# Recurrence output copied out of PSUM at once, its transposes one chunk later

## The chip, the cores and the metric

The kernel runs on one core of a Trainium2 chip. Times are microseconds (us) of one launch on the device. The matrix engine is PE (TensorE), the vector engine DVE, the scalar engine ACT, GpSimd POOL, and SP (SyncE) issues DMAs. The metric is the median of the launch times: 2477.68 us over 3 runs (2475.45 to 2480.0).

## The reference

It is a two-layer encoder trunk on 1024 tokens of width 1024, in float32. Layer 0 mixes by a gated MLP and pooling, layer 1 by RWKV-7; a SwiGLU feed-forward network (FFN) follows each, and a norm ends it. The change lies in RWKV-7, per head of 64:

```
def step(state, inp):                      # one token, 16 heads
    r_t, w_t, k_t, v_t, a_t, b_t = inp
    sa = einsum('bhvk,bhk->bhv', state, a_t)
    state = state * w_t + sa * b_t + v_t * k_t      # outer products
    return state, einsum('bhvk,bhk->bhv', state, r_t)
...
y = wkv7_scan(rh, decay, kh, vh, -kk, kk * ah)
y = (y - mean(y)) * rsqrt(var(y) + GN_EPS)          # per token and head
y = y * ln_w + ln_b + bonus
return (y * g) @ w_o
```

The FFN is `(silu(hn @ w_gate) * (hn @ w_up)) @ w_down`, with a hidden width of 2816.

## The kernel before

The tokens are worked in two halves of 512 (h = 0, 1). Every big product splits both float32 operands into a high and a low part and sums three matmuls: lines 344 to 346 (`mm3`), each 128x128 weights against 512 columns. A weight tile of 512 KB is loaded (`raw`), ACT rounds it to the high part (line 143: `whi`, for the down projection `wdhi`), and DVE subtracts it to get the low part (line 144: `wlo`, `wdlo`). ACT also issues the loads (line 113). One group of the FFN has three hidden tiles: six gate and up tiles of 24 matmuls each, then three down tiles with 72 matmuls together.

The recurrence of a half (`recur`) runs beside an FFN stage of dense matmuls. Eight chunks of 64 tokens follow each other, all heads at once, in small matmuls (line 1176). In the rows, a chunk (`burst`) reads in this order:

- `sm<-XT,w` (`below2`), evicted to `XT` by ACT and DVE;
- `sm<-uv,gt` (`own`), evicted to `akv` by ACT; `sm<-S,ar`, added to `akv` as `Q` by DVE;
- `sm<-ar,bk` (`gram`, two halves for the next chunk), evicted to `gt` by DVE;
- `sm<-Q,XT`, evicted to `uv` by ACT and DVE;
- `yp<-S,ar`, and later `yp<-uv,gt`: the output of the chunk, in PSUM;
- `sm<-uv,bkt`, added to the state by DVE (`Q<-S`, `S`);
- `sm<-ident,bk` (`flip_bk`), evicted to `bkt` by ACT; `sm<-XT,gt` (`below`), evicted to `w` by ACT and DVE.

Two chunks share one PSUM tile `yp` of two banks, and there is one such tile. All `sm` results share three PSUM banks in turn. After every second chunk `post` takes the statistics of `yp` (line 1353), a power on POOL gives the scale, ACT normalizes 16 heads out of `yp` (line 1370), DVE and POOL apply gain and bonus, PE transposes the result (`sm<-ident,ysb`, 1 and then 7), and DVE gates it into `gch` (line 1390), which SP writes out. The small matmuls keep their written order (`ordered`). Where dense matmuls stand between them, and how the work of ACT, DVE and SP is interleaved, is set by a scheduler that runs on its own estimates when the kernel is built; the engines then run their lists in that order.

Of the kernel before, what the change touches and what calls it, by code (L numbers as in the profile page):

```python
# [11 lines left out]
AF = mybir.ActivationFunctionType  # L12
ALU = mybir.AluOpType
# [3 lines left out]
P = 128  # L17
# [19 lines left out]
def tile_trunk(  # L37
# [8 lines left out]
    act, dve, pool, pe, sp = nc.scalar, nc.vector, nc.gpsimd, nc.tensor, nc.sync  # L46
    x = x.flatten_outer_dims()
    out = out.flatten_outer_dims()
# [31 lines left out]
    ident = const.tile([P, P], F32, name="ident")  # L80
# [9 lines left out]
    C_MIX, C_FFN, C_MU, C_W0, C_A0, C_KK, C_KA, C_RK, C_LNB = 0, 16, 32, 80, 88, 96, 104, 112, 120  # L90
# [3 lines left out]
    def col(c):  # L94
        return vec[:, c : c + 1]
# [229 lines left out]
    def pst(tag):  # L325
        t, n = psum["tags"][tag]
        return psum["pool"].tile([P, HT], F32, tag=t, bufs=n, name=t)
# [148 lines left out]
    o = auxt()  # L476
# [675 lines left out]
    def recur(h, wp):  # L1152
# [5 lines left out]
        def wt(tag, bufs, shape):  # L1158
            return wp.tile(shape, F32, tag=tag, bufs=bufs, name=tag)
# [12 lines left out]
        def ordered(f, *args, **kw):  # L1172

            if last:
                with tc.issue_after(last.pop()):
                    i = f(*args, **kw)  # L1176
            else:
                i = f(*args, **kw)
            last.append(i.ins)
# [47 lines left out]
        def flip_bk(c):  # L1227
            bk = C[c][1]
            bkt = wt("bkt", 1, [P, 8, P])
            for q in range(2):  # L1230
                o = pst("sm").rearrange("p (a b) -> p a b", b=P)
                for j in range(4):
                    ordered(pe.transpose, o[:, j, :], bk[:, q * 4 + j].rearrange("p a b -> p (a b)"), ident)
                act.activation(bkt[:, q * 4 : q * 4 + 4, :], o, AF.Copy)
            return bkt
# [41 lines left out]
        def burst(c, bkt, w1):  # L1277

            ar, _, uv, gt, _, XT = C[c]
            cg, S0, more = h * 8 + c, S[0], c < 7  # L1280
            below2(c, w1)
            akv = own(c)
            oq = smt()
            each(oq, lambda r, p: ar[rows[r], p, 0, :], lambda r, p: S0[rows[r], p, :])
            Q = wt("Q", 1, [P, 8, 64])
            dve.tensor_tensor(out=Q, in0=akv, in1=oq, op=ALU.add)
            yield 0.1
            if more:
                gram(c + 1, 0)
                yield 0.1  # L1290
            ou = smt()
            each(ou, lambda r, p: XT[rows[r], p, :], lambda r, p: Q[rows[r], p, :])
            act.activation(uv[rows[0], :, 0, :], ou[rows[0]], AF.Copy)
            dve.tensor_copy(uv[rows[1], :, 1, :], ou[rows[1]])
            yield 0.1
            if c % 2 == 0:
                ypair[0] = psum["pool"].tile([P, 2, 8, 64], F32, tag="y", bufs=1, name="yp")

            yp = ypair[0][:, c % 2]
            for p in range(8):  # L1300
                for r in range(2):
                    mm(
                        yp[rows[r], p, :], ar[rows[r], p, 1, :], S0[rows[r], p, :], start=p == 0, stop=False,
                        skip_group_check=True,
                    )
            yield 0.1
            if more:
                gram(c + 1, 1)
                yield 0.1
            if cg < NCH - 1:  # L1310
                Sn = state_d if c == 7 else wt("S", 2, [P, 8, 64])
                os_ = smt()
                each(os_, lambda r, p: bkt[:, p, r * 64 : r * 64 + 64], lambda r, p: uv[:, p, r, :])
                tS = wt("Q", 1, [P, 8, 64])
                dve.tensor_tensor(out=tS, in0=S0, in1=os_, op=ALU.add)
                dve.tensor_tensor(out=Sn, in0=tS, in1=bc(pct[:, cg, :].unsqueeze(2), [P, 8, 64]), op=ALU.mult)
                S[0] = Sn
                yield 0.1
            for p in range(8):
                for r in range(2):  # L1320
                    mm(
                        yp[rows[r], p, :], gt[:, p, r, 64:128], uv[:, p, r, :], start=False, stop=p == 7,
                        skip_group_check=True,
                    )
            C.pop(c)
            yield 0.1
            if more:
                bkt = flip_bk(c + 1)
                if c < 6:
                    load(c + 2)  # L1330
                yield 0.1
                w1 = below(c + 1)
                yield 0.1
            return bkt, w1

        def post(jj):
            yp = ypair[0]
            j = h * 4 + jj
            gch = wt("gch", 1, [P, 8, P])
            sp.dma_start(gch, g_d[h][:, :, jj * P : (jj + 1) * P])  # L1340
            vch = wt("vch", 1, [P, 2, 8, 64])
            for r in range(2):
                sp.dma_start(
                    vch[rows[r]].rearrange("t c p d -> t c (p d)"),
                    v_d[h][jj * P : (jj + 1) * P, r].rearrange("(c t) p d -> t c (p d)", t=64),
                )
            v16 = vch.rearrange("t c p d -> t (c p) d")
            b16 = bon[:, 2 * j : 2 * j + 2, :].rearrange("t c p -> t (c p)")
            pool.tensor_tensor(out=v16, in0=v16, in1=bc(b16.unsqueeze(2), [P, 16, 64]), op=ALU.mult)
            st = wt("st", 1, [P, 2, 8, 6])  # L1350
            for r in range(2):
                for p in range(8):
                    dve.bn_stats(out=st[:, r, p, :], in_=yp[:, r, p, :])
            sts = st.rearrange("p a b s -> p (a b) s")
            mean, dm, var = (wt(n, 1, [P, 16]) for n in ("mean", "dm", "var"))
            me, mo, ve, vo = (sts[:, :, i] for i in (1, 4, 2, 5))
            dve.tensor_tensor(out=mean, in0=me, in1=mo, op=ALU.add)
            dve.tensor_tensor(out=dm, in0=me, in1=mo, op=ALU.subtract)
            dve.tensor_tensor(out=var, in0=ve, in1=vo, op=ALU.add)
            dve.scalar_tensor_tensor(out=dm, in0=dm, scalar=16.0, in1=dm, op0=ALU.mult, op1=ALU.mult)  # L1360
            dve.tensor_tensor(out=var, in0=var, in1=dm, op=ALU.add)
            dve.tensor_scalar(out=var, in0=var, scalar1=1.0 / 64, scalar2=GN_EPS, op0=ALU.mult, op1=ALU.add)
            rsqrt(var)
            dve.scalar_tensor_tensor(out=mean, in0=mean, scalar=-0.5, in1=var, op0=ALU.mult, op1=ALU.mult)
            yield 0.3
            ysb = wt("ysb", 1, [P, 2, 8, 64])
            for r in range(2):
                for p in range(8):
                    i = r * 8 + p
                    act.activation(  # L1370
                        ysb[:, r, p, :], yp[:, r, p, :], AF.Identity, scale=var[:, i : i + 1], bias=mean[:, i : i + 1]
                    )
            yield 0.3
            for q, eng in enumerate((dve, pool)):
                eng.tensor_tensor(out=ysb[:, q], in0=ysb[:, q], in1=lnw, op=ALU.mult)
                eng.tensor_tensor(out=ysb[:, q], in0=ysb[:, q], in1=vch[:, q], op=ALU.add)
            yield 0.3
            yield 0.3
            for q in range(2):
                o = pst("sm")  # L1380
                for i in range(4):
                    p = 4 * q + i // 2 * 2
                    ordered(
                        pe.transpose, o[:, i * P : (i + 1) * P], ysb[:, i % 2, p : p + 2, :].rearrange("t p d -> t (p d)"), ident
                    )
                ov = o.rearrange("p (q c r t) -> p q r c t", q=2, c=2, r=2)
                for i in range(4):
                    m = q * 4 + i
                    g = gch[:, m, :].rearrange("p (c t) -> p c t", c=2)
                    dve.scalar_tensor_tensor(  # L1390
                        out=g, in0=ov[:, i // 2, i % 2], scalar=col(C_LNB + m), in1=g, op0=ALU.add, op1=ALU.mult,
                    )
                yield 0.5
            sp.dma_start(y_d[h][:, :, jj * P : (jj + 1) * P], gch)

        load(0)
        load(1)
# [8 lines left out]
        for c in range(8):  # L1406
            bkt, w1 = yield from burst(c, bkt, w1)
            yield BURST / 2
            if c % 2 == 1:
                yield from post(c // 2)  # L1410
            yield BURST / 2

    def out_proj(h, ys, after=None):
        for m in range(KT):
# [220 lines left out]
```

## Time and profile before

| | |
|---|---|
| median of 3 runs | 2477.68 us |
| the profiled execution, its own time | 2477.63 us |
| its span, first to last instruction | 2475.9 us |
| PE busy | 2406.4 us, 97% |
| DVE, ACT, POOL busy | 1382.7, 912.1, 244.6 us |
| mean granted clock of PE | 0.989 |

The slices of the page show PE at 9 tenths nearly everywhere. The first recurrence lies at about 933 to 1178 us, the second at about 1640 to 1885 us. A row of a timeline gives the start, the length, the engine, the line, the operation, out<-in, and in brackets how long the engine had been idle and what ended that. Matmuls overlap, so the step from one start to the next is what one costs.

### The profile page before, as it was taken

The page shows a single profiled execution, that of the slowest core. Times are in us where ns is not written, and L with a number is a line of the kernel's source. Part 1 is how long each engine was busy: PE and PEld are TensorE (multiplying, and loading weights), DVE is VectorE, ACT ScalarE, POOL GpSimd, SP SyncE. Part 2 cuts the span into 40 slices and gives each one's busy share as a digit, 9 for nine tenths or more (in the row PEclk, how much of TensorE's full clock was granted, in tenths as well). Part 3 has the DMA queues.
Part 4 walks back from the last instruction along what each step waited for, and adds up shares of the span by engine and source line. Part 5 has one row for each costly group of instructions (what it writes and reads, how often), then busy time and mean ns, then how long its engine had stood idle before and what let it go on. Part 6 is the DMA issues. An engine that isn't in the chain of part 4 may idle for free.

```text
span 2475.9 us, 37980 instructions
## 1 busy us (share of the span) xinstructions
PE 2406.4 (97%) x15735; PEld 1977.5 (80%) x15735; DVE 1382.7 (56%) x2126; ACT 912.1 (37%) x1369; POOL 244.6 (10%) x262
## 2 busy tenths in 40 slices
PE   8999999999999998999999999989999999999998
PEld 7888888888878787888878777778878778888887
DVE  6445634444875874655548847856555446444443
ACT  6233422222664432432325754433232324322223
POOL 0200000000014400211000133201111000000001
PEclk9999999999999999999999999999999999999999
DMA  5123433323355577542434465695444322433231
GB/s 179 49 60 89 150 102 102 119 86 94 109 176 139 140 208 202 156 127 70 135 112 143 153 168 134 191 234 140 119 128 128 111 85 75 147 102 118 87 98 56
DMA packets 436396, 310.69 MB, mean 125 GB/s; under 512 B 93376, under 2 KB 395584, under 8 KB 435456
## 3 DMA queue, kind: packets, MB, share of 16 engines
q10 hardware_dynamic: 297280, 210.53, 28.6%
q1 hardware_dynamic: 138944, 97.75, 13.8%
q8 instruction: 123, 2.02, 0.3%
q14 instruction: 49, 0.40, 0.1%
HBM read 254.68 MB, written 53.54 MB: 124 GB/s over the span
## 4 chain that ended last, share of the span: by engine, by line
PE 82%; DMA 6%; DVE 5%; ACT 2%; issue 2%; POOL 2%; SPq 0%; ACTq 0%; POOLq 0%; DVEq 0%
PE mm L344 22%; PE mm L345 22%; PE mm L346 22%; PE sm L1176 5%; DMA raw<-y_d 1%; DVE wlo L144 1%; PE yp L1176 1%; DMA raw<-in_ffn_w_down_dram 1%; DMA lnw<-in_rwkv_ln_w_dram 1%; ACT whi L143 1%; PE aux L1097 1%; PE mm L511 1%; PE mm L512 1%; PE mm L513 1%; PE aux L1098 1%
## 5 line engine op out<-in xcount | busy, mean ns | idle before, releaser
L345 PE MATMUL mm<-alo,whi 128*128 128x512 f32 x1952 | 766.7, 393 | 0.9 <-issue 0.8
L346 PE MATMUL mm<-ahi,wlo 128*128 128x512 f32 x1952 | 765.4, 392 | 1.7 <-DVE wlo L144 1.7
L344 PE MATMUL mm<-ahi,whi 128*128 128x512 f32 x1952 | 765.8, 393 | 0.8 <-ACT whi L143 0.8
L143 ACT ACTIVATE whi<-raw 128x1024 fp32r<-128x1024 f32 x288 | 304.6, 1059 | 744.7 <-PE mm L345 605.3
L144 DVE TENSOR_TENSOR wlo<-raw,whi 128x1024 fp32r<-128x1024 f32 x288 | 359.1, 1248 | 289.5 <-ACT whi L143 270.1
L346 PEld LDWEIGHTS mm<-ahi,wlo 128*128 128x128 f32 x1952 | 367.7, 188 | 82.5 <-issue 3.5
L345 PEld LDWEIGHTS mm<-alo,whi 128*128 128x128 f32 x1952 | 367.7, 188 | 79.9 <-issue 2.9
L344 PEld LDWEIGHTS mm<-ahi,whi 128*128 128x128 f32 x1952 | 367.7, 188 | 79.0 <-issue 2.1
L344 PE MATMUL mm<-hidhi,wdhi 128*128 128x512 f32 x624 | 240.5, 395 | 8.1 <-DVE h L424 3.8
L345 PE MATMUL mm<-hidlo,wdhi 128*128 128x512 f32 x624 | 245.0, 393 | 0.4 <-DVE hidlo L674 0.4
L346 PE MATMUL mm<-hidhi,wdlo 128*128 128x512 f32 x624 | 244.9, 392 | 0.0
L424 DVE TENSOR_TENSOR h<-h,mm 128x512 f32<-128x512 f32 x192 | 129.3, 686 | 149.7 <-PE mm L346 148.5
L143 ACT ACTIVATE wdhi<-raw 128x1024 fp32r<-128x1024 f32 x82 | 86.4, 1057 | 249.7 <-DMA raw<-in_ffn_w_down_dram 164.4
L144 DVE TENSOR_TENSOR wdlo<-raw,wdhi 128x1024 fp32r<-128x1024 f32 x82 | 100.2, 1223 | 112.1 <-ACT wdhi L143 112.0
L670 DVE TENSOR_TENSOR sg<-sg,mm 128x512 f32<-128x512 f32 x88 | 60.3, 686 | 157.1 <-PE mm L346 155.3
L344 PEld LDWEIGHTS mm<-hidhi,wdhi 128*128 128x128 f32 x624 | 117.5, 189 | 36.8 <-DVE h L424 6.4
L345 PEld LDWEIGHTS mm<-hidlo,wdhi 128*128 128x128 f32 x624 | 117.8, 189 | 25.7 <-DVE hidlo L674 1.3
L346 PEld LDWEIGHTS mm<-hidhi,wdlo 128*128 128x128 f32 x624 | 117.8, 189 | 24.9
L424 DVE TENSOR_TENSOR hA<-hA,mm 128x512 f32<-128x512 f32 x72 | 48.8, 686 | 77.2 <-PE mm L346 77.0
L349 POOL TENSOR_TENSOR nrs<-nrs,small 128x4 f32<-128x4 f32 x8 | 10.0, 1244 | 667.2 <-DVE nrs L371 667.2
L674 DVE TENSOR_TENSOR hidlo<-sg,hidhi 128x512 fp32r<-128x512 f32 x88 | 65.7, 748 | 10.0 <-ACT hidhi L673 10.0
L344 PE MATMUL mm<-xhi,whi 128*128 128x512 f32 (+1 forms) x160 | 65.3, 408 | 0.0
(299 smaller groups left out, 2886.3 us busy)
## 6 DMA issues: line engine op xcount, KB each, us to landing
raw<-in_ffn_w_gate_dram ACTq DMA_DIRECT2D x88, 512.0 KB
raw<-in_ffn_w_up_dram ACTq DMA_DIRECT2D x88, 512.0 KB
raw<-in_ffn_w_down_dram ACTq DMA_DIRECT2D x88, 512.0 KB
raw<-in_ab_w_in_dram ACTq DMA_DIRECT2D x16, 512.0 KB
raw<-in_ab_w_out_dram ACTq DMA_DIRECT2D x16, 512.0 KB
raw<-in_rwkv_w_r_dram ACTq DMA_DIRECT2D x16, 512.0 KB
raw<-in_rwkv_w_k_dram ACTq DMA_DIRECT2D x16, 512.0 KB
ar_d<-ar SPq DMA_DIRECT2D x16, 512.0 KB
```

The costliest lines, as they stand in the source:

```text
L143: act.activation(hi, src, AF.Copy)
L144: (eng or dve).tensor_tensor(out=lo, in0=src, in1=hi.bitcast(F32), op=ALU.subtract)
L344: pe.matmul(o, whi, xhi, start=first, stop=False)
L345: pe.matmul(o, whi, xlo, start=False, stop=False)
L346: pe.matmul(o, wlo, xhi, start=False, stop=last)
L424: dve.tensor_tensor(out=H[h][:, m, :], in0=H[h][:, m, :], in1=o, op=ALU.add)
L511: pe.matmul(ops[j], xhi[:, k, sl], whi[:, kk], start=(k == 0), stop=False)
L512: pe.matmul(ops[j], xhi[:, k, sl], wlo[:, kk], start=False, stop=False)
L513: pe.matmul(ops[j], xlo[:, k, sl], whi[:, kk], start=False, stop=(k == KT - 1))
L670: dve.tensor_tensor(out=s, in0=s, in1=o, op=ALU.mult)
L674: dve.tensor_tensor(out=lo, in0=s, in1=hi.bitcast(F32), op=ALU.subtract)
L1176: i = f(*args, **kw)
```

## The change

`post` begins with two ACT copies that take both halves of `yp` to the SBUF tile `ysb`; statistics and normalization then read `ysb`, and the normalization is in place. The transposes, the gating and the write of `y_d` move to a closure, `turn_out`, which the next chunk calls between `flip_bk` and `below`; the last one is called after the loop. Shortened:

```
             if more:
                 bkt = flip_bk(c + 1)
+                if turned:
+                    turned.pop()()
                 if c < 6:
                     load(c + 2)
...
         def post(jj):
-            yp = ypair[0]
+            ysb = wt("ysb", 1, [P, 2, 8, 64])
+            for r in range(2):
+                act.activation(ysb[:, r], ypair[0][:, r], AF.Copy)
...
-                    dve.bn_stats(out=st[:, r, p, :], in_=yp[:, r, p, :])
+                    dve.bn_stats(out=st[:, r, p, :], in_=ysb[:, r, p, :])
...
-                        ysb[:, r, p, :], yp[:, r, p, :], AF.Identity, scale=var[:, i : i + 1], bias=mean[:, i : i + 1]
+                        ysb[:, r, p, :], ysb[:, r, p, :], AF.Identity, scale=var[:, i : i + 1], bias=mean[:, i : i + 1]
...
-            yield 0.3
-            for q in range(2):
-                o = pst("sm")
...
-                yield 0.5
-            sp.dma_start(y_d[h][:, :, jj * P : (jj + 1) * P], gch)
+            def turn_out():
+                for q in range(2):
+                    o = pst("sm")
...
+                sp.dma_start(y_d[h][:, :, jj * P : (jj + 1) * P], gch)
+            turned.append(turn_out)
...
+        turned.pop()()
+        yield 1.0
```

The number of instructions on PE stays the same. The order of the lists changes from the third chunk of each recurrence on. First PE, end of the seventh chunk of the first recurrence; before:

```order
L1176 MATMUL sm<-uv,bkt 64x64 x16
L1176 MATMUL yp<-uv,gt 64x64 x16
L1176 MATMUL sm<-ident,bk 128x128 x8
L1176 MATMUL sm<-XT,gt 32x32 x16
L345 MATMUL mm<-alo,whi 128x512
```

And with the change, at the same place:

```order
L1176 MATMUL sm<-uv,bkt 64x64 x16
L1176 MATMUL yp<-uv,gt 64x64 x16
L1176 MATMUL sm<-ident,bk 128x128 x8
L1176 MATMUL sm<-ident,ysb 128x128 x4
L346 MATMUL mm<-ahi,wlo 128x512
```

Four transposes of the pair before now follow the flips; 14 dense matmuls, four more transposes, one dense matmul and `sm<-XT,gt` come behind them.

Second ACT, where the loads and splits of the second group's down tiles stand (`raw`, `wdhi`); before, in the sixth chunk:

```order
L1274 ACTIVATE akv<-sm 128x512
L143 ACTIVATE whi<-raw 128x1024
L673 ACTIVATE hidhi<-sg 128x512
L113 DMA raw<-in_ffn_w_down_dram 128x1024
L1293 ACTIVATE uv<-sm 64x8x64
L143 ACTIVATE wdhi<-raw 128x1024
L113 DMA raw<-in_ffn_w_down_dram 128x1024
L143 ACTIVATE wdhi<-raw 128x1024
L1234 ACTIVATE bkt<-sm 128x512 x2
```

With the change, in the seventh chunk:

```order
L1274 ACTIVATE akv<-sm 128x512
L143 ACTIVATE whi<-raw 128x1024
L673 ACTIVATE hidhi<-sg 128x512
L113 DMA raw<-in_ffn_w_down_dram 128x1024
L143 ACTIVATE wdhi<-raw 128x1024
L1293 ACTIVATE uv<-sm 64x8x64
L113 DMA raw<-in_ffn_w_down_dram 128x1024
L143 ACTIVATE wdhi<-raw 128x1024
L113 DMA raw<-in_ffn_w_down_dram 128x1024
L143 ACTIVATE wdhi<-raw 128x1024
L1234 ACTIVATE bkt<-sm 128x512 x2
```

`uv` now stands behind the first down tile's split, and `bkt` behind all three.

Third DVE, the same places; before:

```order
L1223 TENSOR_TENSOR gt<-sm,gm 128x4x128 x2
L1294 COPY uv<-sm 64x8x64
L144 TENSOR_TENSOR wdlo<-raw,wdhi 128x1024
L1223 TENSOR_TENSOR gt<-sm,gm 128x4x128 x2
L1315 TENSOR_TENSOR Q<-S,sm 128x512
L1316 TENSOR_TENSOR S<-Q,pct 128x512
L1353 BN_STATS st<-yp 128x6 x16
L144 TENSOR_TENSOR wdlo<-raw,wdhi 128x1024
```

With the change:

```order
L1223 TENSOR_TENSOR gt<-sm,gm 128x4x128 x2
L144 TENSOR_TENSOR wdlo<-raw,wdhi 128x1024
L1294 COPY uv<-sm 64x8x64
L1223 TENSOR_TENSOR gt<-sm,gm 128x4x128 x2
L144 TENSOR_TENSOR wdlo<-raw,wdhi 128x1024
L1315 TENSOR_TENSOR Q<-S,sm 128x512
L1316 TENSOR_TENSOR S<-Q,pct 128x512
L144 TENSOR_TENSOR wdlo<-raw,wdhi 128x1024
L1397 SCALAR_TENSOR_TENSOR gch<-sm,vec,gch 128x128 x4
```

Here `uv`, the state update `Q<-S` and the gating `gch` each stand behind one more `wdlo`.

## Rows read from the trace of the kernel before

**Rows 1.** The page, part 1: busy time, share of the span, instructions.
```profile
PE 2406.4 (97%) x15735; PEld 1977.5 (80%) x15735; DVE 1382.7 (56%) x2126; ACT 912.1 (37%) x1369; POOL 244.6 (10%) x262
```
**Rows 2.** Stretches of both recurrences: us, busy PE, PEld, DVE, ACT, POOL, PEclk, DMA, GB/s.
```profile
998.00:1178.00 180.00, 177.28 (x2389) 148.09 (x2388) 104.15 (x207) 64.32 (x130) 30.52 (x22) 1.00 0.42 120
1705.00:1885.00 180.00, 174.75 (x2339) 145.28 (x2338) 102.15 (x205) 62.76 (x127) 29.25 (x22) 0.99 0.41 117
```
**Rows 3.** Waits of PE, 998 to 1178: us in total, times, longest us.
```profile
PE sm L1176 <- DVE gt L1223: 1.9, 2, 1.7
```
**Rows 4.** Waits of PE, 1705 to 1885.
```profile
PE sm L1176 <- DVE gt L1223: 2.1, 2, 2.0
...
PE sm L1176 <- DVE ysb L1376: 1.3, 1, 1.3
```
**Rows 5.** Timeline of PE, the fourth chunk of the first recurrence.
```profile
1031.69 0.69 PE L1176 MATMUL sm<-XT,w 32*32 32x32 f32 x32
...
1040.92 1.10 PE L1176 MATMUL yp<-uv,gt 128*64 128x64 f32 x32
1041.96 1.09 PE L1176 MATMUL sm<-ident,bk 128*128 128x128 f32 x8
...
1043.36 0.40 PE L345 MATMUL mm<-alo,whi 128*128 128x512 f32 x1
1043.68 0.69 PE L1176 MATMUL sm<-XT,gt 32*32 32x32 f32 x32
1044.31 0.50 PE L346 MATMUL mm<-ahi,wlo 128*128 128x512 f32 x1
1044.64 0.40 PE L344 MATMUL mm<-ahi,whi 128*128 128x512 f32 x1
1044.87 0.39 PE L345 MATMUL mm<-alo,whi 128*128 128x512 f32 x1
```
**Rows 6.** Timeline of ACT, three down tiles in the second recurrence.
```profile
1793.49 0.60 ACT L1274 ACTIVATE akv<-sm 128x512 f32<-128x512 f32 x1 [0.70 <-PE sm L1176]
...
1797.70 0.35 ACTq L113 DMA_DIRECT2D raw<-in_ffn_w_down_dram  x1
...
1801.51 1.06 ACT L143 ACTIVATE wdhi<-raw 128x1024 fp32r<-128x1024 f32 x1 [2.69 <-DMA raw<-in_ffn_w_down_dram]
1803.85 0.35 ACTq L113 DMA_DIRECT2D raw<-in_ffn_w_down_dram  x1
1808.36 1.06 ACT L143 ACTIVATE wdhi<-raw 128x1024 fp32r<-128x1024 f32 x1 [5.79 <-DMA raw<-in_ffn_w_down_dram]
1810.70 0.33 ACTq L113 DMA_DIRECT2D raw<-in_ffn_w_down_dram  x1
...
1815.63 1.06 ACT L143 ACTIVATE wdhi<-raw 128x1024 fp32r<-128x1024 f32 x1 [3.05 <-DMA raw<-in_ffn_w_down_dram]
```
**Rows 7.** Timeline of DVE, the same place.
```profile
1799.50 0.69 DVE L1294 COPY uv<-sm 64x512 f32<-64x512 f32 x1
1802.60 1.23 DVE L144 TENSOR_TENSOR wdlo<-raw,wdhi 128x1024 fp32r<-128x1024 f32 x1 [2.40 <-ACT wdhi L143]
```
**Rows 8.** Timeline of PE, the same place.
```profile
1804.60 1.25 PE L1176 MATMUL sm<-ident,bk 128*128 128x128 f32 x8 [1.96 <-DVE gt L1223]
...
1807.00 0.63 PE L345 MATMUL mm<-alo,whi 128*128 128x512 f32 x1
1807.43 0.63 PE L346 MATMUL mm<-ahi,wlo 128*128 128x512 f32 x1
```
**Rows 9.** The chain, two other down tiles: start, us, what.
```profile
1090.15 3.54 DMA raw<-in_ffn_w_down_dram
...
1717.66 5.07 DMA raw<-in_ffn_w_down_dram
```
**Rows 10.** Timelines of ACT and DVE: the normalization and one half of the gating.
```profile
1049.45 4.84 ACT L1370 ACTIVATE ysb<-yp,mean,var 128x64 f32<-128x64 f32 x16 [1.89 <-DVE mean L1364]
...
1715.37 1.13 DVE L1390 SCALAR_TENSOR_TENSOR gch<-sm,vec,gch 128x128 f32<-128x128 f32 x4 [0.29 <-PE sm L1176]
```

More of the change, by code (lines that the diff above doesn't have):

```diff
@@ L1334, in burst @@
             return bkt, w1
+        turned = []
         def post(jj):
-            yp = ypair[0]
+            ysb = wt("ysb", 1, [P, 2, 8, 64])
+            for r in range(2):
+                act.activation(ysb[:, r], ypair[0][:, r], AF.Copy)
             j = h * 4 + jj
@@ L1365, in post @@
             yield 0.3
-            ysb = wt("ysb", 1, [P, 2, 8, 64])
             for r in range(2):
@@ L1377, in post @@
             yield 0.3
-            yield 0.3
-            for q in range(2):
-                o = pst("sm")
[L1381 to L1392, printed above, removed]
-                yield 0.5
-            sp.dma_start(y_d[h][:, :, jj * P : (jj + 1) * P], gch)
+            def turn_out():
+                for q in range(2):
+                    o = pst("sm")
+                    for i in range(4):
+                        p = 4 * q + i // 2 * 2
+                        ordered(
+                            pe.transpose, o[:, i * P : (i + 1) * P],
+                            ysb[:, i % 2, p : p + 2, :].rearrange("t p d -> t (p d)"), ident,
+                        )
+                    ov = o.rearrange("p (q c r t) -> p q r c t", q=2, c=2, r=2)
+                    for i in range(4):
+                        m = q * 4 + i
+                        g = gch[:, m, :].rearrange("p (c t) -> p c t", c=2)
+                        dve.scalar_tensor_tensor(
+                            out=g, in0=ov[:, i // 2, i % 2], scalar=col(C_LNB + m), in1=g, op0=ALU.add, op1=ALU.mult,
+                        )
+                sp.dma_start(y_d[h][:, :, jj * P : (jj + 1) * P], gch)
+            turned.append(turn_out)
         load(0)
```

## The prediction

> **What bounds the kernel now.** First the engine totals on the page: PE is busy 97% of the span [rows 1], so a change can gain only where PE stands idle beside the changed code. Next the windows of the two stretches that lie between the end of the first pair and the last `post`: PE is busy for 177.28 and 174.75 of 180 us at a granted clock of 1.00 and 0.99 [rows 2]. That leaves 2.72 + 5.25 = 7.97 us of idle time in both. Then PE's waits in the same stretches: the flips of a chunk, `sm<-ident,bk`, wait for DVE's `gt` for 1.9 and 2.1 us (one long wait in each) [rows 3, 4], and the first transpose of a pair waits 1.3 us for `ysb` [rows 4]. These 5.3 us can be touched; the other 2.7 are short waits and issue time. Last, the timelines of ACT, DVE and PE around the 1.96 us wait show its cause. ACT issues a down tile's load and splits it 3.81 us later, for 1.06 us; DVE's `wdlo` takes 1.23 us and only then goes the next load into the same buffer, at 1803.85 [rows 6, 7]. A load, its split and the low part are one link of about 6.1 us, and a group has three links in series, with landings of 3.81, 4.51 and 4.93. `gt` stands in DVE's list behind the first `wdlo`; that is how the 1.96 us come about [rows 8]. The next two links cost PE nothing, since it is then in the 64 to 76 dense matmuls that follow `post` in the list before. A dense matmul steps by 0.23 us (1044.64 to 1044.87) [rows 5], so such a run covers 15 to 17 us.
>
> After the 1.96 us wait the next dense matmuls step by 0.43 and last 0.63 us instead of 0.39, the lower level of the clock (1.2 GHz against 2.4 GHz) [rows 5, 8]; I count seven of them: 7 x (0.43 - 0.22) = 1.5 us.
>
> **The change part by part.** PE's work stays the same in kind and number. What is removed: `yp` is free after two copies instead of after the 16 normalizations, whose end lies 1049.45 + 4.84 - 1041.96 = 12.3 us behind the last matmul of the pair [rows 5, 10]. The odd chunk may start its `yp` sooner, so the order puts the chunks closer: I count 627 dense matmuls within the first recurrence before and 554 after, 615 and 528 in the second. The old first links and the wait for `ysb` go, with the slow matmuls behind one: -(5.3 + 1.5) = -6.8 us.
>
> Cost on ACT and DVE: 8 pairs x 2 copies of 128x512, each like `akv` at 0.60 us [rows 6], are 9.6 us of an engine busy 37% [rows 1]; the statistics wait for them, but `turn_out` comes a chunk later, so they lie beside PE's work. If that cover went, a pair would cost 1.2 us. SP's write of `gch` comes a chunk later, and its reload of `gch` and `vch` behind it; nothing in PE's list waits for them before the next pair's transposes. I cost these at nothing.
>
> More switches: the dense matmuls within the recurrences stand in 37 and 33 runs instead of 32 and 31, so 7 more. A switch costs 0.32 us into the small ones (1043.36 to 1043.68) and 0.33 out (1044.31 to 1044.64) instead of twice 0.23 [rows 5]: 7 x 0.19 = +1.3 us.
>
> What is moved is the large term. Without the long runs behind `post`, the down tiles of four groups now lie in the third and seventh chunk of the first recurrence and the fourth and eighth of the second, and the recurrence's own evictions stand behind them, as the order shows: `uv` behind the first `wdlo`, `Q<-S` behind the second, `bkt` behind the third split, `gch` behind the third `wdlo`. The freeing of PSUM banks hangs on these too: the first four transposes take the bank that `Q<-S` reads, the next four the bank of the first `bkt`. I work out the seventh chunk, from T, the last `yp` matmul of the sixth.
>
> ACT and DVE: the normalizations run from T + 7.5 to T + 12.3 [rows 10]; then come `XT`, `akv` (0.60), the last gate split (1.06) and its low part, so the first down load goes at T + 15.9. It lands after 3.81, split 1.06, `wdlo` 1.23: T + 22.0, and `uv` (0.69) T + 22.7. The second link, landing 4.51, ends at T + 28.9 and `Q<-S` at T + 29.6. The third, landing 4.93, ends its split at T + 34.9, `bkt` (0.6) T + 35.5 [rows 6, 7].
>
> PE: flips and `below` 1.8, then 19 + 29 + 1 dense matmuls at 0.23 (11.3), and the small matmuls of a chunk up to `sm<-uv,bkt`: 10.27 (1031.69 to 1041.96) less its 7 dense (1.6) and the last two steps (2.2), 6.5 [rows 5]. PE wants `uv` at about T + 19.5 and waits 3.2. Then `sm<-uv,bkt`, `yp` and the flips, 3.0: it wants the bank of `Q<-S` at T + 25.7 and waits 3.9. Four transposes and 14 dense matmuls later, 3.9, it wants that of `bkt` at T + 33.5 and waits 2.0. The sum is 9.1 us. In the same way the third chunk of the first recurrence gives 0.7 + 0.3 + 1.8 = 2.8 (37 dense matmuls stand ahead of its `uv`), the fourth of the second 2.2, since its chain has a link less ahead of what PE asks for, and the eighth 0.5. New waits: 9.1 + 2.8 + 2.2 + 0.5 = +14.6 us.
>
> The clock falls after some of them: I take two of the dips of [rows 8], 2 x 1.5 = +3.0.
>
> Sum: -6.8 + 1.3 + 14.6 + 3.0 = +12.1 us. The profiled execution took 2477.63 us (span 2475.9), as good as the median of 2477.68. So 2489.7; I say 2490.
>
> The landing is what I know least. The rows have 3.54 to 5.07 us for this tile [rows 9]. With all at 3.54 the same walk gives 9.0 us of waits, and without dips -6.8 + 1.3 + 9.0 = +3.5, 2481; with all at 5.07 it gives 20.8, and with four dips (6.0) +21.3, 2499. I take the landings of [rows 6], which lie between.
>
> The rows' landings are longer than a rule of the Trainium skill would make them: "DMA: Bandwidth & Descriptors", section "Anatomy of one DMA", gives a fixed 2.0 us and the bytes by 436 GB/s, for loads that GpSimd issues; for 512 KB I estimate 3.2 us by it. By that figure the walk gives about 8.6 us of waits and the sum, without dips, 2481. The loads here are issued by ACT, and the traced ones took 3.54 at the least [rows 9], so the measurement decides.
>
> **The rivals.** *No change that can be told.* PE comes later to the second and third link than I reckon, because the first wait shifts it but not the chain, and each of the four groups shows its first link alone, about 2 us as in [rows 3, 4]: -6.8 + 1.3 + 4 x 2 = +2.5, 2480. For it: before, just one link of a group showed. Against it: the cover that hid the others is what the change takes out. *Faster.* The chains end before PE asks: the 12.3 us by which `yp` held the chunk are what the long runs were for, and the dense matmuls moved behind the recurrence run without a wait. Then all of -6.8 is kept against 1.3 for the switches: 2472, and 2470 if half of the other 2.7 us of idle time goes too. For it: before, DVE and ACT are busy 104 and 64 of 180 us [rows 2], so lists alone, not load, make them late. Against it: three serial links are some 19 us, longer than a chunk without its dense matmuls. *Much slower.* Each new wait of over 1.5 us brings a dip and landings are the long ones, since loads of gate tiles now stand close to those of `gch`, `vch` and the next chunk: 2499 as above; it decides from landings of about 5 us on. For it: 5.07 in the trace. Against it: most are shorter.
>
> **How the numbers follow.** A measurement of this kernel can tell about 0.2%, 5 us. My forecast, some waits of 2 to 4 us in the four chunks, has a chance of 0.5, from 2481 to 2499; no change 0.26; faster 0.13; much slower 0.11. Of my own case nearly all lies above 2482.6. That makes faster 0.13, same 0.25, slower 0.62. The range of 2474 to 2502 leaves out the better part of the faster case and a tail above.
>
> **What would show it.** Right: PE waits for `uv` and `Q<-S` of DVE and `bkt` of ACT in the seventh chunk of the first recurrence, 2 to 4 us each, with a `wdlo` or a `wdhi` just ahead of the evicting instruction and a load ahead of that; smaller ones in the three other chunks; matmuls at half clock behind them; no wait for `ysb`; the recurrences end some 17 and 20 us earlier, as 73 and 87 dense matmuls move behind them. The waits outside the two recurrences stay. Wrong: PE as dense as before in these chunks, or landings under 3.5 us, or the long waits at places where nothing of the down tiles is queued.

## The result and the profile after

The changed kernel takes 2488.49 us (median of 5 runs, 2485.25 to 2492.59) against 2477.68 before: 1.0044 of before, 95% interval 1.0029 to 1.0058. That is +10.8 us; the forecast was 2490 with a range of 2474 to 2502. The profiled execution took 2489.14 us, 11.5 more than the profiled one of before.

All kernels below have the same 15735 matmuls, and outside the recurrences, but for a handful, in the same order. So the time between two matmuls of the same number can be compared from kernel to kernel. In us against before:

| stage (matmuls from, to) | change | late only | copies only | cleared | before, cleared |
|---|---|---|---|---|---|
| up to the first recurrence (0 to 4340) | +0.4 | +2.0 | +3.2 | +2.1 | -0.1 |
| first recurrence (to 7700) | +14.5 | +14.3 | +2.0 | +0.2 | -0.6 |
| between (to 9950) | +0.2 | +2.1 | -2.0 | +0.3 | +0.5 |
| second recurrence (to 13250) | -4.3 | +5.0 | +0.3 | -4.6 | -6.2 |
| behind it (to 13800) | +0.7 | -0.1 | +7.6 | +0.1 | +1.6 |

From matmul 13800 to 15700, close to the end, each takes 423.15 us. The first column is the changed kernel; the others are experiments. Each column is one execution: in the first stage no list of an engine differs yet, and still the columns run from -0.1 to +3.2, so a difference of 3 us in one stage tells nothing. The loss lies in the first recurrence (3.0 of its 14.5 us up to matmul 4540, where no list differs yet either), and the second one gains.

The page's totals after the change, against [rows 1]:

```profile
PE 2413.2 (97%) x15735; PEld 1981.8 (80%) x15735; DVE 1376.6 (55%) x2126; ACT 924.4 (37%) x1385; POOL 239.0 (10%) x262
```

and the two windows of [rows 2], with two short ones in the seventh chunk:

```profile
998.00:1178.00 180.00, 170.99 (x2339) 142.41 (x2338) 97.96 (x209) 65.50 (x133) 29.50 (x23) 0.97 0.39 114
1705.00:1885.00 180.00, 177.24 (x2542) 148.47 (x2535) 106.72 (x242) 68.79 (x139) 30.76 (x25) 1.00 0.46 134
...
1112.00:1119.00 7.00, 2.11 (x39) 1.24 (x34) 2.59 (x4) 1.54 (x2) 1.90 (x1) 0.96 0.48 144
1119.50:1125.00 5.50, 5.45 (x72) 5.06 (x72) 3.03 (x4) 1.06 (x1) 0.00 (x0) 0.50 0.29 98
```

and one in the third chunk:

```profile
1019.43:1022.84 3.41, 3.41 (x53) 3.29 (x48) 0.54 (x1) 0.75 (x1) 0.00 (x0) 0.50 0.36 133
```

PE is idle for 9.0 us in the first window (2.7 before) and 2.8 in the second (5.3 before). PE's waits in the first, against [rows 3]:

```profile
PE sm L1176 <- DVE uv L1294: 7.9, 2, 4.8
PE sm L1176 <- DVE gt L1223: 0.6, 2, 0.5
PE sm L1176 <- ACT bkt L1234: 0.5, 1, 0.5
```

The wait for `gt` has shrunk to 0.6 us; two for `uv` are new, 3.1 us in the third chunk and 4.8 in the seventh. In the second window nothing exceeds 1.1 us. The seventh chunk on ACT:

```profile
1102.13 5.43 ACT L1375 ACTIVATE ysb<-ysb,mean,var 128x64 f32<-128x64 f32 x16 [5.76 <-DVE mean L1370]
...
1111.40 0.35 ACTq L113 DMA_DIRECT2D raw<-in_ffn_w_down_dram  x1
1116.46 1.06 ACT L143 ACTIVATE wdhi<-raw 128x1024 fp32r<-128x1024 f32 x1 [6.04 <-DMA raw<-in_ffn_w_down_dram]
1117.42 0.57 ACT L1293 ACTIVATE uv<-sm 64x512 f32<-64x512 f32 x1
1118.81 0.35 ACTq L113 DMA_DIRECT2D raw<-in_ffn_w_down_dram  x1
1122.17 1.06 ACT L143 ACTIVATE wdhi<-raw 128x1024 fp32r<-128x1024 f32 x1 [4.18 <-DMA raw<-in_ffn_w_down_dram]
```

on DVE:

```profile
1109.67 1.70 DVE L144 TENSOR_TENSOR wlo<-raw,whi 128x1024 fp32r<-128x1024 f32 x1
...
1117.55 1.23 DVE L144 TENSOR_TENSOR wdlo<-raw,wdhi 128x1024 fp32r<-128x1024 f32 x1 [4.38 <-ACT wdhi L143]
1118.81 0.69 DVE L1294 COPY uv<-sm 64x512 f32<-64x512 f32 x1
```

and on PE:

```profile
1093.73 1.09 PE L1176 MATMUL sm<-ident,bk 128*128 128x128 f32 x8
...
1119.56 1.97 PE L1176 MATMUL sm<-uv,bkt 128*64 128x64 f32 x32 [4.80 <-DVE uv L1294]
...
1123.16 1.97 PE L1176 MATMUL sm<-ident,bk 128*128 128x128 f32 x8
...
1129.50 0.66 PE L1176 MATMUL sm<-ident,ysb 128*128 128x128 f32 x4 [0.46 <-ACT bkt L1234]
```

Read from below: PE's `sm<-uv,bkt` waits for DVE's `uv`, which stands behind `wdlo`, that waits for `wdhi`, that for a load of 5.06 us issued at 1111.40, behind the last gate split, behind the normalization. After the wait the flips take 1.97 us instead of 1.09: the granted clock is 0.50 from 1119.5 to 1125 (the last window above), the lower of the two levels (1.2 GHz), after PE had done 2.1 us of work in 7. In the third chunk it is 0.50 from 1019.43 to 1022.84, behind the wait of 3.1 us.

### The profile page after: what moved, and what is told of

Read it like the earlier page. It is cut to its first block, busy times and chain, and to the rows that moved or that the text cites. A ratio compares the mean times of both kernels' runs of the same rounds, so it can differ in the third digit from the quotient of the medians.

```text
span 2487.4 us, 38011 instructions
## 1 busy us (share of the span) xinstructions
PE 2413.2 (97%) x15735; PEld 1981.8 (80%) x15735; DVE 1376.6 (55%) x2126; ACT 924.4 (37%) x1385; POOL 239.0 (10%) x262
## 4 chain that ended last, share of the span: by engine, by line
PE 80%; DMA 7%; DVE 6%; ACT 3%; issue 2%; POOL 1%; SPq 0%; ACTq 0%; POOLq 0%; DVEq 0%
PE mm L344 22%; PE mm L345 22%; PE mm L346 22%; PE sm L1176 4%; DMA raw<-in_ffn_w_down_dram 2%; DVE wlo L144 1%; DMA raw<-y_d 1%; PE yp L1176 1%; DMA lnw<-in_rwkv_ln_w_dram 1%; ACT whi L143 1%; DMA XT<-xi_d 1%; PE aux L1097 1%; PE mm L511 1%; PE mm L512 1%; PE mm L513 1%
## 5 line engine op out<-in xcount | busy, mean ns | idle before, releaser
L674 DVE TENSOR_TENSOR hidlo<-sg,hidhi 128x512 fp32r<-128x512 f32 x88 | 60.2, 685 | 9.3 <-ACT hidhi L673 9.3
```

Source lines behind the costliest of these rows:

```text
L674: dve.tensor_tensor(out=lo, in0=s, in1=hi.bitcast(F32), op=ALU.subtract)
```

## The experiments

Three theories were put against each other. L: the loss comes from down tiles whose splits wait for loads ahead of the recurrence's evictions, in the lists of ACT and DVE. C: from the 16 copies and the normalization in place. S: from the closer packing itself, by more switches and the lower clock. Ratios are to the kernel before, run on the same chip in the same rounds (its median there 2479.5 to 2480.0).

**Each half alone.** The copies only:

```
+            ysb = wt("ysb", 1, [P, 2, 8, 64])
+            for r in range(2):
+                act.activation(ysb[:, r], ypair[0][:, r], AF.Copy)
...
```

with statistics and normalization from `ysb`, and the transposes in `post` as before.

> The copies out of PSUM are made at once, but the transposes stay where they were before the change. Theory L (the loss comes from down tiles whose splits wait for loads ahead of the recurrence's own evictions): the order has 68 to 87 dense matmuls behind each pair again and the down tiles beside them, so PE has no wait for uv over 1 us and the time is 2471 to 2480 us, about 2476. Theory C (the loss comes from the 16 copies and the normalization in place on ACT): as with the whole change, 2486 us or more. Theory S (the loss comes from more switches between small and dense matmuls and from the lower clock): 72 dense runs instead of 63 in both recurrences, 9 x 0.19 = 1.7 us, about 2479.

Measured: 2489.57 us, 1.0041 (1.0029 to 1.0054). L's number fails. C has the number but not the place: there is no wait for `uv`, as L has it, and by the table most of the loss lies behind the second recurrence, +7.6 us. It is taken up below.

The late transposes only: `turn_out` as in the change, statistics and normalization from `yp`, no copy.

> The transposes are made one chunk later, but statistics and normalization read PSUM as before and no copy is made. Theory L: the chunks stand as close as with the whole change (519 and 497 dense matmuls within the recurrences), in the third chunk of the first recurrence uv still stands behind a wdlo, in the seventh no more; so of the two waits of 3.3 and 5.2 us the first stays, the second goes with a dip of 1.5, and the second recurrence gets one or two of about 2 us at its third and eighth chunk: 2480 to 2488 us, about 2484. Theory C: without the copies as before, 2478. Theory S: 68 dense runs, near 2487.

Measured: 2500.63 us, 1.0085 (1.0071 to 1.0099), worse than anything expected. PE's waits in the first and in the second window:

```profile
PE sm L1176 <- DVE uv L1294: 4.2, 1, 4.2
PE sm L1176 <- ACT bkt L1234: 4.1, 2, 3.2
PE sm L1176 <- DVE Q L1315: 1.4, 1, 1.4
...
PE sm L1176 <- DVE gt L1223: 4.7, 2, 4.5
PE sm L1176 <- DVE Q L1315: 3.8, 1, 3.8
```

These add up to 9.7 us in the third chunk of the first recurrence, all three links of one group, and, without the short wait for `gt`, to 8.3 in that of the second, two links. L had these places right (it named the eighth chunk too, where nothing shows) and took only the first link. C is out as the main cause, since there are no copies here. And the dense matmuls within the recurrences are 519 and 497 here, as few as with the change (554, 528), but 677 and 653 with the copies alone: the chunks are packed by the moved transposes, not by the earlier release of `yp`.

**The lists put right, all else kept.** First, a group's splits queued behind `uv`:

```
+    ends, LATE = {}, {("d", 0, 1, f): (0, c) for f, c in ((7, 2), ..., (13, 6), ...)}
...
+        ready[i] = hi, lo; [tc.add_manual_dep(x.ins, y.ins.name, NOSYNC) for x, y in zip(two, ends[LATE[key]])] if key in LATE else 0
```

(an edge that sets the order on an engine and adds no wait).

> The whole change, with the splits of two groups of down tiles queued behind the eviction of uv in the third and seventh chunk of the first recurrence. Theory L: both waits for uv (3.3 and 5.2 us) go, with about 1.5 us of lower clock; a wdlo still stands before gt and Q<-S in the third chunk, which gives back about 2 us there: 2477 to 2484 us, about 2480. Theories C and S: the copies are all there, and 64 dense runs are fewer than 70 by 6 x 0.19 = 1.1 us, so 2486 to 2489.

Measured: 2477.73 us, 0.9992 (0.9984 to 1.0001) where the change has 1.0044. The edge acted in the third chunk; the second group that it names is not the one of the seventh. That one left the seventh chunk by itself, since the lists behind an edge are laid anew. Then the same edges from the state update and the last `bkt` of a chunk, in both recurrences:

```
+    ends, LATE = {}, {("d", l, 1 - l, f + i): (l, c) for l, f, c in ((0, 7, 2), (0, 13, 6), (1, 5, 2), (1, 11, 6)) for i in range(3)}
...
+                ends[h, c] = [dve.tensor_tensor(out=Sn, in0=tS, in1=bc(pct[:, cg, :].unsqueeze(2), [P, 8, 64]), op=ALU.mult)]
...
+            ends[h, c - 1] = [last_bkt] + ends.get((h, c - 1), []); return bkt
```

> The whole change, with the splits of the down tiles queued behind the state update and the flips' evictions of the third and seventh chunk in both recurrences, so that no split of a down tile stands before an eviction of uv, S or bkt. Theory L: no wait over 2 us is left in the chunks, 2473 to 2480 us, about 2476, at or below the kernel before. Theories C and S: 2486 to 2489, since copies and the close packing (528 dense matmuls in each recurrence, 34 runs each) are all there.

Measured: 2475.85 us, 0.9986 (0.9977 to 0.9995). The lists have no down split ahead of `uv`, `Q<-S` or `bkt` in these chunks, and PE's waits in the first and second window are:

```profile
PE sm L1176 <- DVE gt L1223: 1.1, 2, 0.9
...
PE sm L1176 <- DVE gt L1223: 1.5, 3, 1.1
```

The first recurrence is at +0.2 us instead of +14.5. All copies are there, and the packing too (528 dense matmuls in each recurrence, 34 runs each): C and S as the main cause are out.

**What the copies are worth once the lists are clear.** The same edges on the late transposes without copies.

> The transposes one chunk later without copies, with the down tiles' splits queued behind the third and seventh chunk's state update as in the cleared version of the change. Theory L: the waits for uv, bkt and Q<-S of the version with late transposes alone (some 17 us) go: 2475 to 2481 us, about 2478, at most 3 us over the cleared version with copies, since yp is held some 12 us by the normalization. Theory C (copies cost): below the cleared version with copies by 2 us or more.

Measured: 2476.44 us, 0.9983 (0.9975 to 0.9992), with the same waits gone: 24 us below the same code without the edges. Copies or none, the cleared kernels are the same within their intervals, as L had it; C's 2 us are not there.

**The kernel before, cleared.** Its waits for `gt` [rows 3, 4] have the same form, so edges for one group of each recurrence, behind the sixth chunk's state update and `bkt`:

```
+    LATE = {("d", l, 1 - l, f + i): (l, c) for l, f, c in ((0, 10, 5), (1, 8, 5)) for i in range(3)}
```

> The kernel before, with the splits of one group of down tiles in each recurrence queued behind the state update and the flips' evictions of the sixth chunk, where its waits of 1.9 and 2.1 us for gt were. Theory L: both waits go, with 1.5 us of lower clock, 2 to 5 us below the kernel before; with that the two orders, packed and not, would be within 2 us of each other. A rival (the packing itself gains what the cleared version of the change gained): no difference from the kernel before.

Measured: 2473.67 us, 0.9974 (0.9963 to 0.9984), the lowest of all and 6.4 us below the kernel before, a little more than L's 2 to 5. The waits in the first and second window, against 1.9 and 2.1:

```profile
PE sm L1176 <- DVE gt L1223: 0.2, 1, 0.2
...
PE sm L1176 <- DVE gt L1223: 0.7, 3, 0.4
```

The rival (that the packing gains) falls: unpacked and packed (0.9974 and 0.9986) cannot be told apart when both are cleared. By the table the gain lies in the second recurrence (-6.2 us); in the first the wait of 1.7 us went too, yet that stage is only 0.6 us shorter.

**The landing or the place.** Twelve down loads left out:

```
+    SAME = [("d", l, 1 - l, f) for l in range(2) for f in range(7 - 2 * l, 13 - 2 * l)]
...
+        raw = raws[i - 1] if plan[i][0] in SAME else wst.tile([P, D], F32, tag="raw", name="raw")
```

> The whole change, without the loads of twelve down tiles (two groups in each recurrence); their splits take the tile that was loaded before them, so a part of the FFN's weights is not computed with. In the seventh chunk of the second recurrence two wdlo still stand directly before uv and one before Q<-S, as in the third and seventh chunk of the first recurrence with the whole change. Theory L, in the form that the landing is the price: no wait for uv, Q<-S or bkt over 1 us, 2471 to 2478 us. If the place in the list alone did it (1.06 of split and 1.23 of subtraction each, without a landing), about 2 us of wait at that uv, 2478 to 2482. Theories C (copies) and S (packing: 71 dense runs): 2486 or more.

Measured: 2484.03 us, 1.0017 (1.0006 to 1.0028); none of the numbers holds. In the first recurrence no wait over 0.2 us is left behind its start (2.3 us below before), but there the lists changed too (the down tiles' splits stand ahead of the normalization in the third chunk and behind the state update in the seventh), so this says nothing of the landing. In the second (5.1 us above before) PE waits in the third chunk for `gt`, behind three `wdlo` and a `wlo`, 3.5 us, and still for `uv` in the seventh:

```profile
PE sm L1176 <- DVE gt L1223: 3.9, 3, 3.5
PE sm L1176 <- DVE uv L1294: 3.4, 1, 3.4
```

The timeline of the seventh chunk, of all engines:

```profile
1801.35 5.42 ACT L1375 ACTIVATE ysb<-ysb,mean,var 128x64 f32<-128x64 f32 x16
...
1806.67 2.00 ACT L143 ACTIVATE wdhi<-raw 128x1024 fp32r<-128x1024 f32 x2
...
1807.75 3.67 DVE L144 TENSOR_TENSOR wdlo<-raw,wdhi 128x1024 fp32r<-128x1024 f32 x2 [0.99 <-ACT wdhi L143]
...
1808.20 2.13 POOL L1381 TENSOR_TENSOR ysb<-ysb,vch 128x512 f32<-128x512 f32 x1
...
1811.45 0.69 DVE L1294 COPY uv<-sm 64x512 f32<-64x512 f32 x1
...
1812.20 0.98 PE L1176 MATMUL sm<-uv,bkt 128*64 128x64 f32 x26 [3.39 <-DVE uv L1294]
```

No load is in this chain: normalization, two splits, two subtractions, `uv`, and 3.4 us of wait. The two subtractions take 3.67 us instead of twice 1.23, beside POOL's `tensor_tensor`; without these 1.2 us the wait would be about the 2 us expected of the place alone (an estimate). So a landing is not needed; the place behind two down tiles is enough when the normalization of the pair stands ahead of them. That the landing makes one tile as dear as two here, and three links in series the 8 to 10 us of the late transposes, is read from the chains (loads of 5.06 us with the change); no run takes the landing away and keeps the lists.

**Where the copies alone lose.** Behind the second recurrence PE waits for gate and up tiles (the row names ACT's `sg`, which stands behind the split of such a tile):

```profile
PE mm L344 <- ACT sg L662: 5.5, 2, 3.1
```

while a residual of 2 MB (`h<-h_d`) is reloaded. First its instruction was moved behind the FFN groups in the source:

```
-    reload(hb_pool, 1, h_d[1, 1])
     ys = open_act(("y", 1), b)
     drive(ffn(1, 0, hnA, f, G1A[2], between=take_act(("y", 1))))
+    reload(hb_pool, 1, h_d[1, 1])
```

> The copies alone, with the reload of 2 MB for the residual behind the second recurrence issued after the FFN groups there and not ahead of them. In the copies' version the stretch behind the second recurrence took 7.6 us more than before, where PE waits for gate and up tiles whose loads run beside that reload. If the reload is what delays them: 5 to 8 us below the version with the copies alone, 2482 to 2485. If it is the order of ACT's list there: no change, 2489. If the copies in the recurrences cost it: no change.

Measured: 2490.65 us, 1.0036 (1.0023 to 1.0049). The edit did not do what it was meant for: SP still issued the reload at 1905.83, and a gate load issued at 1905.89 was split only at 1916.30:

```profile
1905.89 0.41 ACTq L113 DMA_DIRECT2D raw<-in_ffn_w_gate_dram  x1
...
1916.30 1.06 ACT L143 ACTIVATE whi<-raw 128x1024 fp32r<-128x1024 f32 x1 [9.36 <-DMA raw<-in_ffn_w_gate_dram]
```

It tells nothing of the cause. Then with an order that holds, on ACT:

```
+                with tc.issue_after(did[("u",1,0,15)].ins):
+                    act.dma_start(H[1], h_d[1, 1])
```

> The copies alone, with the 2 MB reload behind the second recurrence queued on ACT behind the split of the second up tile there; the lists of PE and DVE stay as in the copies' version. The version of before with the reload emitted later did not start it later (it still ran beside the gate load, which landed after 10.3 us). If the reload beside these loads is the price: the wait of 3 to 4.6 us at about 1916 us goes, 2484 to 2487 us, with the second wait of about 2.4 us left. If not: 2489 to 2491 us.

Measured: 2484.19 us, 1.0015 (1.0004 to 1.0025), 5.4 us below the copies alone. The gate load comes back in 5.4 us, and the reload follows at 1913.41:

```profile
1905.15 0.39 ACTq L113 DMA_DIRECT2D raw<-in_ffn_w_gate_dram  x1
...
1910.57 1.06 ACT L143 ACTIVATE whi<-raw 128x1024 fp32r<-128x1024 f32 x1 [4.37 <-DMA raw<-in_ffn_w_gate_dram]
```

PE's wait there:

```profile
PE mm L344 <- ACT sg L662: 1.8, 1, 1.8
```

The stage behind the second recurrence is at +0.7 us instead of +7.6. So this loss is a collision of that reload with loads of weights, at a moment that the copies' order chose. Before, the reload (issued at 1888.37) ran beside loads too, and an up tile issued at 1890.58 was split only at 1901.24, but PE waited 0.5 us for `sg` there. What remains (+4.7 us) is in the first recurrence, +7.7 us in this execution and +2.0 in that of the copies alone, with the same lists there. They part at two places. Between matmuls 4540 and 5000 it is 3.6 us: PE waits 2.0 us for `XT`, and the clock is 0.50 for 3.4 us behind it. DVE's `wlo` ahead of `XT` is late because POOL's addition began just before it; with the copies alone DVE began first, and POOL was the late one. POOL and DVE with the reload moved, then DVE and POOL with the copies alone:

```profile
963.28 1.90 POOL L1351 TENSOR_TENSOR vch<-vch,bon 128x1024 f32<-128x1024 f32 x1 [48.72 <-DMA vch<-v_d]
963.35 2.92 DVE L144 TENSOR_TENSOR wlo<-raw,whi 128x1024 fp32r<-128x1024 f32 x1 [2.22 <-ACT whi L143]
...
965.04 1.23 DVE L144 TENSOR_TENSOR wlo<-raw,whi 128x1024 fp32r<-128x1024 f32 x1 [0.93 <-ACT whi L143]
965.11 2.92 POOL L1351 TENSOR_TENSOR vch<-vch,bon 128x1024 f32<-128x1024 f32 x1 [48.10 <-DMA vch<-v_d]
```

In the sixth chunk it is 2.2 us: PE waits 3.4 us for `gt` instead of 2.7, behind two `wdlo`, and the clock is 0.51 for 3.4 us behind that. So the 5.7 us are no work of the reload; the execution of the edit that failed, again with the same lists there, has +7.9.

**The recurrence's start.** PE waits 4 to 7 us there for `gt`, again behind subtractions of weight tiles, in every kernel so far. One more set of edges, on the cleared kernel before and on the cleared change (-1 stands for the first `gt` and `bkt` of a recurrence; the change also names its seventh chunk's groups by their numbers now):

```
-    ... for l, f, c in ((0, 10, 5), (1, 8, 5)) ...
+    ... for l, f, c in ((0, 4, -1), (1, 2, -1), (0, 10, 5), (1, 8, 5)) ...
-    ... for l, f, c in ((0, 7, 2), (0, 13, 6), (1, 5, 2), (1, 11, 6)) ...
+    ... for l, f, c in ((0, 4, -1), (1, 2, -1), (0, 7, 2), (1, 5, 2), (0, 10, 6), (1, 8, 6)) ...
```

> The cleared version of the kernel before, with the first group's splits also queued behind the first gt and bkt at the start of each recurrence, where PE waits 4 to 5 us for gt. Theory L for this place: the long wait goes, 3 to 8 us below the cleared version, 2466 to 2471 us. A rival: in this stretch the DMA engines are 97% busy, so the dense matmuls wait for the same tiles a little later, and the time stays at 2472 to 2476 us.

> The whole change, with the splits of the down tiles of three groups in each recurrence queued behind the evictions at its start, in its third and in its seventh chunk. Theory L with the start: 2468 to 2473 us; if the start is bound by the DMA engines, 2474 to 2477, as the cleared version. If the change itself (copies and late transposes) is worth something once the queues are clear, it is below the twice cleared version of the kernel before by 2 us or more; otherwise they are within 3 us or it is slower.

Measured: 2478.86 us, 0.9996 (0.9986 to 1.0007), and 2474.56 us, 0.9980 (0.9970 to 0.9990). The rival of the first holds in its mechanism, though the time lies above its range too. The wait for `gt` is gone, and a dense matmul waits in its place; in the kernel before with both sets of edges:

```profile
PE mm L344 <- DVE h L424: 4.3, 1, 4.3
```

The window of that start (columns as in [rows 2]):

```profile
925.00:957.00 32.00, 30.61 (x239) 24.33 (x239) 10.40 (x13) 7.90 (x11) 1.91 (x1) 1.00 1.04 282
```

The DMA engines are busy all the time in it (share 1.04; before, 1.05), which fits the rival: the tiles come no sooner, whatever the lists say. Its median is no better than that of before, 5 us over the singly cleared one, although its profiled execution took 2472.16; what the 12 runs (2472.16 to 2485.40) differ by was not found. The change, cleared twice, is 4.3 us below the kernel before, cleared twice, which by the expectation is a gain of its own. But it is not below the kernel before, cleared once (0.9980 against 0.9974), nor is the change, cleared once (0.9986). Two sets of edges on the kernel before lie 5 us apart, so these runs do not settle whether the change is worth anything by itself.

## Why the prediction was right

The time, its sign and the place came out as forecast, and the cause was shown by experiment: without the down tiles ahead of the evictions, the loss is gone with copies, late transposes and packing all in place. That the total came within 2 us is in part luck, as the terms show:

- **What goes.** The waits of -5.3 us and the dip went, as said; the second recurrence, in which 3.4 of them lay, gained 4.3 (in one execution; forecast: -1.8, by 2.7 of new waits less 3.4, a dip of 1.5 and 0.4 of switches).
- **What comes.** 14.6 us of new waits were forecast. In the windows' terms 9.0 came in the first recurrence (7.9 + 0.6 + 0.5) and 2.7 in the second (1.1 + 0.7 + 0.5 + 0.4; forecast 2.7). In the seventh chunk the three waits were to be 3.2, 3.9 and 2.0; they were 4.8, none over 0.5, and 0.5. The first is larger, since the load went at T + 17.7 (1111.40 - 1093.73) and not T + 15.9, and landed after 5.06 us. The others are smaller, since the next two came after 3.36 and 3.38 (the rows had 4.51 and 4.93), and PE at the lower clock reached its questions later. The third chunk has 3.1 for 2.8 in all, the fourth of the second recurrence 2.2 (1.1 for `akv`, 0.4 and 0.7) for 2.2, the eighth 0.5 for 0.5. So the waits fell 3 us short of the forecast; with late transposes alone all three links did show.
- **The clock.** Two dips of 1.5 us were taken, and two came, in the third and the seventh chunk of the first recurrence. They cost more: PE is busy at half clock for 3.41 us in the one and 5.45 in the other (windows above), so about 4.4 us (an estimate, half of both) for 3.0. By its terms the forecast has +14.0 for the first recurrence (11.9 of new waits, 3.0 of clock and 1.0 of switches, less 1.9). Measured terms give 12.5 (9.0 - 1.9 of waits, 4.4 of clock, 1.0 of switches taken as forecast); the +14.5 of the table holds 3.0 more from the start of the recurrence, where no list differs. So the forecast of this stage was met in part by luck.
- **The cover.** That copies cost nothing beside PE's work holds only nearly. The normalization, behind the copies, belongs to the chain of the late `uv`, and the load there went 1.8 us later than reckoned: the normalization takes 5.43 us instead of 4.84 [rows 10] and starts 0.9 later, and the subtraction behind it takes 1.70 us instead of 1.23. Where the lists are clear, copies or none are the same within the intervals.
- **The step that failed** is the reason for the packing. The prediction said that `yp`, free after two copies, lets the odd chunk start sooner, and that so the chunks stand closer. The copies alone leave 677 and 653 dense matmuls within the recurrences, more than before; the late transposes alone leave 519 and 497 with `yp` held as long as before. The order, read for the two halves apart, would have told this.
- **The rivals.** "No change" needed the later links to come before PE; in the seventh chunk they nearly did, and the first, at 4.8 us instead of 2, made up for it. "Faster" is what the cleared version shows: -4 us. "Much slower" had its landing (5.06), yet at one link of each group.
- **The landing.** From issue to split, the six down tiles of the two groups took 5.00, 4.14 and 4.53 us, and 5.06, 3.36 and 3.38: within 0.2 us of the rows' range (3.54 to 5.07). The Trainium skill's figure ("DMA: Bandwidth & Descriptors", section "Anatomy of one DMA"), 3.2 us by the estimate in the prediction, is short by 0.2 for two of them and by 1.8 for the two first ones, on which the loss hangs. (The walk by that figure gives 5.3 us in the seventh chunk, and 8.0 in all if the other chunks wait as with 3.54, not 8.6.)

## What to carry to other kernels

An instruction that waits for a load holds all that stands behind it on its engine, so when a change moves work, list for each engine what now stands behind an instruction that waits, and price the whole series of links, not the first. Before a change is credited or blamed, put the lists right: here edges that only set the order were worth 6 us on the kernel before (0.9974; with more of them, 0.9996, nothing) and 14 on the changed one (0.9986 for 1.0044), and whether the change itself is worth anything could not be told. And build the two halves of a change apart, if only to compare their orders.

## What the runs showed of the hardware

- ACT's 16 normalizations took 4.83 or 4.84 us where they read PSUM, in all eight of before, and 5.40 to 5.43 us where they read and write SBUF, in all eight of after.
- DVE's subtraction of 128x1024 slows beside a `tensor_tensor` on POOL: 1.23 us alone, 3.67 us for two while POOL's ran from 1808.20 to 1810.33, 1.70 us beside another. POOL's own took 2.13 us there and 1.28 elsewhere. Where they began 0.07 us apart, the second one paid: DVE 2.92 us behind POOL's 1.90, or POOL 2.92 behind DVE's 1.23. The Trainium skill's "SBUF — State Buffer", section "SBUF: two separate sides", says that a DVE operation with two SBUF inputs and a GpSimd operation exclude each other on a shared pair of ports; these times agree.
- A load of 512 KB, split after 3.4 to 5.1 us in the changed kernel's two groups, took over 10 us beside one reload of 2 MB (1905.89 to 1916.30), and 5.4 us with that reload moved behind it.
